# Two-layer fp32 decoder trunk on one core: five FFN groups instead of three, the second product threaded one matmul at a time through the next group's half-width matmuls

## The chip, the core and the metric

The kernel runs on one core of a Trainium2 chip, in one launch. The metric is device time in microseconds (us), the median of the runs. The engines that matter here are TensorE (PE, matrix products), VectorE (DVE, sums and subtractions), ScalarE (ACT, copies, casts and the silu) and SyncE (SP, which issues the loads of the weights). Each engine works through its own queue in order; an instruction that waits for a semaphore holds up all that stands behind it on its engine.

## The reference

Two identical layers work on x, 512 tokens by 1024 channels, in float32. A layer first mixes tokens (attention, retention and a short convolution, gated and summed); this half is untouched by the change. Then comes the feed-forward part (FFN), which is where everything here happens:

```
h  = rmsnorm(x, norm_ffn_g[l])
gu = einsum('bsd,df->bsf', h, w_ffn_in[l])        # 1024 -> 2 * 2816
g, u = gu[..., :2816], gu[..., 2816:]
g  = causal_dwconv(g, ffn_conv_w[l], ffn_conv_b[l])   # 3 taps along the tokens
x  = x + einsum('bsf,fd->bsd', silu(g) * u, w_ffn_out[l])   # 2816 -> 1024
```

The first product (with w_ffn_in) makes g and u; silu(g) times u is called the activation here; the second product (with w_ffn_out) takes it back to 1024 channels and is added to x.

## The kernel before

**Tiling.** x is kept transposed: eight tiles x[0] to x[7] of 128 channels by 512 tokens. The 2816 inner channels are 22 steps of 128. One step f makes one activation tile, act0 to act21, 128 by 512.

**Precision.** Every float32 operand is kept as two parts, hi (rounded) and lo (the rest). A product is three matmuls (function mm3): hi by hi, hi weights by lo data, lo weights by hi data. So each weight tile that is loaded (raw_...) is cast on ACT to hi_... and subtracted on DVE to lo_... (split_w), and the same is done to each activation tile (split2: ACT makes its hi, DVE its lo). A weight pair of more than 512 columns has three buffers (HL), and those of 512 columns two of their own; raw tiles have four.

**First product.** Steps 0 to 4 are `plain`: two products of eight channel tiles each, 48 matmuls of 512 columns. Meanwhile `halves` makes from the normalised x seven half-width combinations X[k][..., b] (256 columns). Steps 5 to 21 are `seven`: a Strassen scheme with seven products instead of eight, each over four channel tiles, thus 7 x 4 x 3 = 84 matmuls of 256 columns per step. Its weights are sums of quarters of the loaded weight (s31 and s24, on DVE, each split again into h31/l31 and h24/l24), the quarter a11 (fa) and the lower half (fb). It uses two PSUM tiles: in `a` (pa) and `b` (pb) the products are collected one after another, and between them ACT copies partial results to `pad` and `u` and DVE adds to them. Within a step the order is: pa with fa, pb with h31, pa with h24, pb with h24, pa with h31, pb with fb, pa with fb. After the first product into pa, ACT copies it to pad (COPY pad), and the third product, into pa again, waits for that copy. When the step's last product of pb is done, the chain to the activation is: pad plus pb (DVE), the convolution (one ACTIVATE on ACT and two on DVE, into c), silu (ACT, c), u times c (DVE), the cast to act hi (ACT), the subtraction to act lo (DVE). The last product, into pa, is copied to u by ACT in between.

**Second product.** The 22 steps are cut into groups of 5, 9 and 8 (GROUPS). After a group, `rows` goes through the eight tiles d: load and split w_ffn_out for this group and d (w2), width x 3 matmuls of 512 columns over the group's activations into one PSUM tile (p2, group, d), and one DVE operation that adds the tile to x[d] (L888). All PSUM tiles pa, pb, p2 come from one pool of four (`main`); a second pool of four (`aux`) is nearly unused in the FFN. In the last group of the last layer each x[d] is written out.

**Order.** The program's text is not the order on the engines: a scheduler, which plans by its own model of times, moves instructions that do not depend on each other, and loads and splits of weights go first (high priority). So before the change matmuls of `rows` stand between matmuls of `seven` wherever the planner saw a wait coming: p200, p201, p202 (group 0, d = 0, 1, 2) are begun together, and each one's last activation is taken later. Instructions marked keep_in_program_order stay in the order of the text on their engine.

Of the kernel before, what the change touches and what calls it, by code (L numbers as in the profile page):

```python
# [15 lines left out]
ALU = mybir.AluOpType  # L16
# [4 lines left out]
P = 128  # L21
D = 1024
S = 512
DEPTH = 2
KT = D // P
# [2 lines left out]
DFF = 2816  # L28
FT = DFF // P

GROUPS = (5, 9, 8)
HALF = S // 2
BUCKETS = 32
MAX_DIST = 128
# [19 lines left out]
def trunk(ctx, tc, xT, wr, wh, wt, wda, wret, wsc, wo, wf, w2, par, lamp, relb, onehot, mask, rope, gtab, out):  # L54
# [99 lines left out]
    def weights(src, name):  # L154
        return split_w(load_w(src, name), name)

    def mm3(o, a, b, start, stop, more=False):

        T.matmul(o, a[0], b[0], start=start, stop=False, skip_group_check=more)  # L159
        T.matmul(o, a[0], b[1], start=False, stop=False, skip_group_check=more)  # L160
        T.matmul(o, a[1], b[0], start=False, stop=stop, skip_group_check=more)  # L161

    def split(src, hi, lo, g=None):

# [602 lines left out]
    def ffn(l, fp):  # L767
# [59 lines left out]
            V.tensor_tensor(u, u, c, ALU.mult)  # L827
            return split2(u, pairN(f"act{f}{L}"))

        def seven(f):  # L830
            upper, lower = [load_w(wf[l, f, :, b * D : (b + 1) * D], f"f{b}{L}{f}") for b in range(2)]
            a21, a11, a22, a12 = upper[:, :S], upper[:, S:], lower[:, :S], lower[:, S:]
            with tc.high_priority():
                w11 = split_w(a11, f"fa{L}{f}")
                s31 = fp.tile([P, 2, S], F32, tag="sum", name=f"s31{f}{L}", bufs=2)
                V.tensor_tensor(s31[:, 0], a21, a11, ALU.add)
                V.tensor_tensor(s31[:, 1], a21, a22, ALU.add)
                h31, l31 = slotX(f"h31{f}{L}"), slotX(f"l31{f}{L}")
                split(s31, h31, l31)
                s24 = fp.tile([P, 2, S], F32, tag="sum", name=f"s24{f}{L}", bufs=2)  # L840
                V.tensor_tensor(s24[:, 0], s31[:, 1], a11, ALU.add)
                V.tensor_tensor(s24[:, 1], s24[:, 0], a12, ALU.add)
                h24, l24 = slotX(f"h24{f}{L}"), slotX(f"l24{f}{L}")
                split(s24, h24, l24)
                w2212 = split_w(lower, f"fb{L}{f}")
            w22, w12 = [tuple(t[:, b * S : (b + 1) * S] for t in w2212) for b in range(2)]

            def product(o, w, b, start, stop):
                for k in range(KT // 2):
                    sl = slice(k * P, (k + 1) * P)  # L850
                    mm3(o, (w[0][:, sl], w[1][:, sl]), (X[k][:, 0, b], X[k][:, 1, b]), start and k == 0, stop and k == KT // 2 - 1, True)

            a = main(f"pa{f}{L}")[:, :HALF]
            b = main(f"pb{f}{L}")
# [19 lines left out]
            V.tensor_tensor(u, u, c, ALU.mult)  # L874
            return split2(u, pairN(f"act{f}{L}"))

        def rows(grp, f0, act, d):

            ps = main(f"p2{grp}{d}{L}")
            width = len(act)  # L880
            edge = min(width, KT // 2) if width > KT else 0
            for a, b in ((0, edge), (edge, width)):
                if a < b:
                    w = weights(w2[l, d, :, (f0 + a) * P : (f0 + b) * P], f"w2{L}{grp}{d}{a}")
                    for n in range(a, b):
                        sl = slice((n - a) * P, (n - a + 1) * P)
                        mm3(ps, (w[0][:, sl], w[1][:, sl]), act[n], n == 0, n == width - 1)
            V.scalar_tensor_tensor(x[d], ps, -1.0 if grp else 1.0, x[d], ALU.mult, ALU.add)  # L888
            if l == DEPTH - 1 and grp == len(GROUPS) - 1:
                nc.sync.dma_start(out[:, d], x[d])  # L890

        f0 = 0
        todo = list(range(KT // 2))
        for grp, width in enumerate(GROUPS):
            act = []
            for f in range(f0, f0 + width):
                act.append(seven(f) if grp else plain(f))
                if f == 1:
                    late.close()
                if grp == 0 and f and todo:  # L900
                    halves(todo.pop(0))
            for d in range(KT):
                rows(grp, f0, act, d)
            f0 += width

    for l in range(DEPTH):
        layer(l)
# [106 lines left out]
```

## Time and profile before

| | |
|---|---|
| median of 3 runs | 1522.4 us (1522.21 to 1522.44) |
| the profiled execution | 1522.98 us, span on the core 1521.2 us |
| PE busy | 1512.6 us, 8510 matmuls |
| PE weight loads busy | 1338.7 us |
| DVE busy | 1105.0 us |
| ACT busy | 734.0 us |
| FFN of layer 0 on PE | from 413.3 to 766.9 us |
| FFN of layer 1 on PE | from 1167.2 to 1517.3 us |

PE's busy time includes the tail of each pipelined matmul, so consecutive matmuls overlap in it. What a matmul costs is better read from the distance between the starts of two that follow each other. The names in the rows are those of the program without their buffer numbers: p200L<-act4L,hi_w2L is the second product of group 0, tile d = 0, with activation 4. In a row of the time order, a bracket at the end gives the idle time of that engine just before, and what released it.

### The profile page before, as it was taken

How to read it: one execution, taken by the hardware profiler on the slowest of the kernel's cores; microseconds unless marked ns; L12 is line 12 of the kernel's file. 1: busy time of each engine (PE TensorE's matmuls, PEld its weight loads, DVE VectorE, ACT ScalarE, POOL GpSimd, SP SyncE). 2: the span in 40 equal slices, each digit the busy share in tenths (PEclk: the TensorE clock that was granted, in tenths of full speed). 3: DMA queues.
4: the chain of work that ended last, by engine and by line, in shares of the span. 5: the costliest groups of instructions: out<-in, count | busy, mean ns of one | idle time of the engine just before them, and what ended most of it. 6: DMA issues, size and time to landing. Idle time of an engine off the chain costs nothing.

```text
span 1521.2 us, 22083 instructions
## 1 busy us (share of the span) xinstructions
PE 1512.6 (99%) x8510; PEld 1338.7 (88%) x8510; DVE 1105.0 (73%) x2074; ACT 734.0 (48%) x1304; POOL 13.0 (1%) x26
## 2 busy tenths in 40 slices
PE   9999999999999999999999999999999999999998
PEld 7899988888888999899789999888888889988996
DVE  8588787554688995796656887875545889947963
ACT  4555665333454564464425565643333546634641
POOL 1000000000000000000100000000000000000000
PEclk9999999999999999999999999999999999999999
DMA  6322222232323322522322222222322233324322
GB/s 212 115 73 81 86 84 90 76 104 83 106 74 107 118 92 72 169 84 84 131 77 94 74 91 87 83 84 83 106 88 86 79 113 112 97 84 139 111 59 81
DMA packets 51146, 147.24 MB, mean 97 GB/s; under 512 B 5624, under 2 KB 6023, under 8 KB 51041
## 3 DMA queue, kind: packets, MB, share of 16 engines
q1 hardware_dynamic: 50224, 143.38, 28.7%
q0 software_dynamic: 816, 2.46, 0.6%
q8 instruction: 67, 1.10, 0.3%
q14 instruction: 39, 0.31, 0.1%
HBM read 143.70 MB, written 2.11 MB: 96 GB/s over the span
## 4 chain that ended last, share of the span: by engine, by line
PE 97%; DVE 1%; DMA 1%; issue 0%; ACT 0%; SPq 0%; ACTq 0%; DVEq 0%
PE pnrvgL L161 1%; PE pnrvgL L159 1%; PE pnrvgL L160 1%; PE pnrqkL L160 1%; PE pnrqkL L161 1%; PE pnrqkL L159 1%; PE pnh2L L161 1%; PE pnh2L L159 1%; PE pnh3L L160 1%; PE pnh3L L161 1%; PE pnh1L L161 1%; PE pnh2L L160 1%; PE pnh3L L159 1%; PE pnh1L L160 1%; PE pnh1L L159 1%; PE pnh0L L160 1%
## 5 line engine op out<-in xcount | busy, mean ns | idle before, releaser
L150 ACT CAST hi_tL<-raw_tL 128x1024 fp32r<-128x1024 f32 x60 | 62.9, 1049 | 115.3 <-issue 14.7
L150 ACT CAST hi_w2L<-raw_w2L 128x640 fp32r<-128x640 f32 (+2 forms) x64 | 49.1, 782 | 94.0 <-PE p210L L160 11.2
L151 DVE TENSOR_TENSOR lo_tL<-raw_tL,hi_tL 128x1024 fp32r<-128x1024 f32 x60 | 73.4, 1223 | 15.9 <-ACT hi_tL L150 15.5
L151 DVE TENSOR_TENSOR lo_w2L<-raw_w2L,hi_w2L 128x640 fp32r<-128x640 f32 (+2 forms) x64 | 55.8, 888 | 29.5 <-ACT hi_w2L L150 29.5
L150 ACT CAST hi_fbL<-raw_f1L 128x1024 fp32r<-128x1024 f32 x34 | 35.7, 1051 | 32.3 <-PE pa5L L160 5.7
L150 ACT CAST hi_oL<-raw_oL 128x1024 fp32r<-128x1024 f32 x16 | 16.9, 1054 | 58.1 <-issue 18.7
L151 DVE TENSOR_TENSOR lo_fbL<-raw_f1L,hi_fbL 128x1024 fp32r<-128x1024 f32 x34 | 41.6, 1222 | 1.5 <-ACT hi_fbL L150 1.4
L150 ACT CAST hi_faL<-raw_f0L 128x512 fp32r<-128x512 f32 x34 | 21.1, 620 | 30.7 <-DMA raw_f0L<-in_wf 12.8
L151 DVE TENSOR_TENSOR lo_faL<-raw_f0L,hi_faL 128x512 fp32r<-128x512 f32 x34 | 23.4, 689 | 4.0 <-ACT hi_faL L150 3.9
L150 ACT CAST hi_nrvgL<-raw_nrvgL 128x1024 fp32r<-128x1024 f32 x8 | 8.4, 1051 | 29.7 <-PE pnrvgL L161 13.5
L150 ACT CAST hi_fuL<-raw_fuL 128x1024 fp32r<-128x1024 f32 x10 | 10.5, 1054 | 22.9 <-issue 17.1
L151 DVE TENSOR_TENSOR lo_oL<-raw_oL,hi_oL 128x1024 fp32r<-128x1024 f32 x16 | 19.6, 1224 | 2.8 <-ACT hi_oL L150 2.8
L151 DVE TENSOR_TENSOR lo_nrvgL<-raw_nrvgL,hi_nrvgL 128x1024 fp32r<-128x1024 f32 x8 | 9.8, 1226 | 12.4 <-ACT hi_nrvgL L150 12.4
L150 ACT CAST hi_fgL<-raw_fgL 128x1024 fp32r<-128x1024 f32 x10 | 10.5, 1050 | 14.8 <-issue 13.0
L151 DVE TENSOR_TENSOR lo_nh0L<-raw_nh0L,hi_nh0L 128x768 fp32r<-128x768 f32 x8 | 7.7, 958 | 13.1 <-ACT hi_nh0L L150 13.1
L150 ACT CAST hi_bdL<-raw_bdL 128x512 fp32r<-128x512 f32 x16 | 9.9, 618 | 12.6 <-issue 4.2
L150 ACT CAST hi_nrqkL<-raw_nrqkL 128x1024 fp32r<-128x1024 f32 (+1 forms) x9 | 8.4, 948 | 13.9 <-issue 13.9
L151 DVE TENSOR_TENSOR lo_fuL<-raw_fuL,hi_fuL 128x1024 fp32r<-128x1024 f32 x10 | 12.2, 1222 | 2.9 <-ACT hi_fuL L150 2.9
L150 ACT CAST hi_nh0L<-raw_nh0L 128x768 fp32r<-128x768 f32 x8 | 6.7, 838 | 15.2 <-PE pnh0L L161 7.8
L151 DVE TENSOR_TENSOR lo_nrqkL<-raw_nrqkL,hi_nrqkL 128x1024 fp32r<-128x1024 f32 (+1 forms) x9 | 9.9, 1109 | 5.2 <-ACT hi_nrqkL L150 5.2
L151 DVE TENSOR_TENSOR lo_fgL<-raw_fgL,hi_fgL 128x1024 fp32r<-128x1024 f32 x10 | 12.2, 1222 | 0.8 <-ACT hi_fgL L150 0.8
L150 ACT CAST hi_nh3L<-raw_nh3L 128x768 fp32r<-128x768 f32 x8 | 6.7, 838 | 11.5 <-PE ptg16L L160 5.3
(8471 smaller groups left out, 5969.6 us busy)
## 6 DMA issues: line engine op xcount, KB each, us to landing
raw_tL<-in_wt SPq DMA_DIRECT2D x60, 512.0 KB, 3.3
raw_f0L<-in_wf SPq DMA_DIRECT2D x34, 512.0 KB, 3.8
raw_f1L<-in_wf SPq DMA_DIRECT2D x34, 512.0 KB, 3.7
raw_w2L<-in_w SPq DMA_DIRECT2D x32, 320.0 KB, 2.9
raw_oL<-in_wo SPq DMA_DIRECT2D x16, 512.0 KB, 3.4
raw_w2L<-in_w SPq DMA_DIRECT2D x16, 512.0 KB, 3.5
raw_fgL<-in_wf SPq DMA_DIRECT2D x10, 512.0 KB, 4.0
raw_fuL<-in_wf SPq DMA_DIRECT2D x10, 512.0 KB, 4.0
```

Source lines behind the costliest of these rows:

```text
L150: A.copy(h, raw)
L151: V.tensor_tensor(w, raw, h.bitcast(F32), ALU.subtract)
L159: T.matmul(o, a[0], b[0], start=start, stop=False, skip_group_check=more)
L160: T.matmul(o, a[0], b[1], start=False, stop=False, skip_group_check=more)
L161: T.matmul(o, a[1], b[0], start=False, stop=stop, skip_group_check=more)
```

## The change

Groups become 5, 4, 4, 4 and 5 steps. `seven` is cut in two: `sums` (the load and the weight sums with their splits) is made for this step and the next before the step's matmuls, and `seven` proper takes an iterator `other`. `rows` is now such an iterator: it yields after each of its matmuls. After every three half-width matmuls (one `product` step over k) `seven` takes one 512-wide matmul from `other`. All matmuls of both kinds are kept in the order of the text. The p2 tiles come from `aux`, and for groups of four one load of 1024 columns serves two tiles d.

After group 0 the tiles d = 0 to 3 run alone (60 matmuls of 512 columns), with the sums of steps 5 and 6 in between; its tiles 4 to 7 (60 matmuls) go between the matmuls of group 1. The 96 matmuls of groups 1, 2 and 3 each go between those of the following group, which has 28 places per step. The last group's 120 run alone at the layer's end. The matmuls are the same in number and size; the additions to x[d] become 80 instead of 48 in the two layers.

```diff
-GROUPS = (5, 9, 8)
+GROUPS = (5, 4, 4, 4, 5)
+SOLID = 4
...
-    def mm3(o, a, b, start, stop, more=False):
-        T.matmul(o, a[0], b[0], start=start, stop=False, skip_group_check=more)
-        T.matmul(o, a[0], b[1], start=False, stop=False, skip_group_check=more)
-        T.matmul(o, a[1], b[0], start=False, stop=stop, skip_group_check=more)
+    def mm3(o, a, b, start, stop, more=False, queue=False):
+        for i, (p, q) in enumerate(((0, 0), (0, 1), (1, 0))):
+            t = T.matmul(o, a[p], b[q], start=start and i == 0, stop=stop and i == 2, skip_group_check=more)
+            if queue:
+                tc.keep_in_program_order(t)
...
-        def seven(f):
+        def sums(f):
             upper, lower = [load_w(wf[l, f, :, b * D : (b + 1) * D], f"f{b}{L}{f}") for b in range(2)]
...
-                w2212 = split_w(lower, f"fb{L}{f}")
+            return lower, w11, h31, l31, h24, l24
+
+        def seven(f, other, lower, w11, h31, l31, h24, l24):
+            w2212 = split_w(lower, f"fb{L}{f}")
...
-                    mm3(o, (w[0][:, sl], w[1][:, sl]), (X[k][:, 0, b], X[k][:, 1, b]), start and k == 0, stop and k == KT // 2 - 1, True)
+                    mm3(o, (w[0][:, sl], w[1][:, sl]), (X[k][:, 0, b], X[k][:, 1, b]), start and k == 0, stop and k == KT // 2 - 1, True, True)
+                    next(other, None)
...
-        def rows(grp, f0, act, d):
-            ps = main(f"p2{grp}{d}{L}")
...
+        def rows(grp, f0, act, ds):
+            width = len(act)
+            per = KT // width
+            for d0 in range(ds.start, ds.stop, per):
...
+                w = split_w(raw, f"w2{L}{grp}{d0}")
+                for d in range(d0, d0 + per):
+                    ps = aux(f"p2{grp}{d}{L}")
+                    for n in range(width):
+                        sl = slice(((d - d0) * width + n) * P, ((d - d0) * width + n + 1) * P)
+                        for i, (p, q) in enumerate(((0, 0), (0, 1), (1, 0))):
+                            t = T.matmul(ps, w[p][:, sl], act[n][q], start=n == i == 0, stop=n == width - 1 and i == 2)
+                            tc.keep_in_program_order(t)
+                            if n < width - 1 or i < 2:
+                                yield
+                    V.scalar_tensor_tensor(x[d], ps, -1.0 if grp else 1.0, x[d], ALU.mult, ALU.add)
...
+                    yield
...
-                act.append(seven(f) if grp else plain(f))
+                if grp:
+                    for n in (f, f + 1):
+                        if n < FT and n not in made:
+                            made[n] = sums(n)
+                    act.append(seven(f, other, *made[f]))
+                else:
+                    act.append(plain(f))
...
-            for d in range(KT):
-                rows(grp, f0, act, d)
+            run(other)
+            if not grp:
+                for half in (range(SOLID // 2), range(SOLID // 2, SOLID)):
+                    run(rows(grp, f0, act, half))
+                    n = f0 + width + half.start // (SOLID // 2)
+                    made[n] = sums(n)
+            other = rows(grp, f0, act, range(0 if grp else SOLID, KT))
             f0 += width
+        run(other)
```

What this does to the queues is seen at three places. A row gives line, operation, what is written <- what is read, and the size; x2 stands for two that read the same. The lines of the changed kernel are shifted: mm3 is L163, the matmul of `rows` L903.

**1. End of group 0 in layer 0.** On PE, p200 is the first tile of the second product and act4 the group's last activation. Before:

```order
L159 MATMUL p200L_4409<-act3L_4302,hi_w2L_4412 128x512
L160 MATMUL p200L_4409<-act3L_4302,hi_w2L_4412 128x512
L161 MATMUL p200L_4409<-act3L_4302,lo_w2L_4413 128x512
L159 MATMUL p201L_4432<-act0L_4050,hi_w2L_4435 128x512
L160 MATMUL p201L_4432<-act0L_4050,hi_w2L_4435 128x512
L161 MATMUL p201L_4432<-act0L_4050,lo_w2L_4436 128x512
```

and now:

```order
L903 MATMUL p200L_4415<-act3L_4302,hi_w2L_4411 128x512 x2
L903 MATMUL p200L_4415<-act3L_4302,lo_w2L_4412 128x512
L903 MATMUL p200L_4415<-act4L_4391,hi_w2L_4411 128x512 x2
L903 MATMUL p200L_4415<-act4L_4391,lo_w2L_4412 128x512
L903 MATMUL p201L_4438<-act0L_4050,hi_w2L_4434 128x512 x2
```

The matmuls on act4 stood behind all of p201's and p202's on the other activations; now they follow act3 directly. On DVE, between u4 times c4 and the lo part of act4, stood before (xt3 and X3 belong to `halves`):

```order
L827 TENSOR_TENSOR u4L_4388<-u4L_4388,c4L_4359 128x512
L800 TENSOR_TENSOR xt3L_4398<-xn3L_4394 128x256
L167 TENSOR_TENSOR X3L_3928<-xn3L_4394,X3L_3928 128x256
L802 TENSOR_TENSOR xt3L_4398<-xn7L_4396,xn3L_4394 128x256
L167 TENSOR_TENSOR X3L_3928<-xn7L_4396,X3L_3928 128x512
L801 SCALAR_TENSOR_TENSOR xt3L_4398<-xt3L_4398,xn7L_4396 128x256
L167 TENSOR_TENSOR act4L_4391<-u4L_4388,act4L_4391 128x512
```

and now:

```order
L831 TENSOR_TENSOR u4L_4388<-u4L_4388,c4L_4359 128x512
L804 TENSOR_TENSOR xt3L_4398<-xn3L_4394 128x256
L841 TENSOR_TENSOR s315L_4463<-raw_f0L_4455 128x512
L842 TENSOR_TENSOR s315L_4463<-raw_f0L_4455,raw_f1L_4457 128x512
L171 TENSOR_TENSOR X3L_3928<-xn3L_4394,X3L_3928 128x256
L806 TENSOR_TENSOR xt3L_4398<-xn7L_4396,xn3L_4394 128x256
L171 TENSOR_TENSOR X3L_3928<-xn7L_4396,X3L_3928 128x512
L805 SCALAR_TENSOR_TENSOR xt3L_4398<-xt3L_4398,xn7L_4396 128x256
L171 TENSOR_TENSOR act4L_4391<-u4L_4388,act4L_4391 128x512
```

The two weight sums of step 5 (s315) have come in ahead of act4's lo part.

**2. From step 12 to step 13, an end of a new group.** On PE, in the middle of step 13 of layer 0, the second product p220 of the group with act9 to act12 now runs between the half-width matmuls:

```order
L903 MATMUL p220L_5813<-act11L_5630,lo_w2L_5810 128x512
L163 MATMUL pa13L_5801<-X1L_3926,h2413L_5651 128x256 x2
L163 MATMUL pa13L_5801<-X1L_3926,l2413L_5652 128x256
L903 MATMUL p220L_5813<-act12L_5772,hi_w2L_5809 128x512
L163 MATMUL pa13L_5801<-X2L_3927,h2413L_5651 128x256 x2
L163 MATMUL pa13L_5801<-X2L_3927,l2413L_5652 128x256
L903 MATMUL p220L_5813<-act12L_5772,hi_w2L_5809 128x512
```

where, before, step 13's third product ran without any between:

```order
L161 MATMUL pa13L_5643<-X0L_3925,l2413L_5636 128x256
L159 MATMUL pa13L_5643<-X1L_3926,h2413L_5635 128x256
L160 MATMUL pa13L_5643<-X1L_3926,h2413L_5635 128x256
L161 MATMUL pa13L_5643<-X1L_3926,l2413L_5636 128x256
L159 MATMUL pa13L_5643<-X2L_3927,h2413L_5635 128x256
```

So the matmul on act12 stands in the order ten places into step 13, with the rest of pa13 and pb13 behind it. On ACT, the chain of act12 before:

```order
L858 COPY pad_116<-pa13L_5643 128x256
L166 CAST h2413L_5635<-s2413L_5632 128x1024
L309 ACTIVATE c12L_5608<-pad_115,par_110 128x512
L166 CAST act11L_5486<-u11L_5389 128x512
L860 COPY u13L_5645<-pb13L_5644 128x256
L150 CAST hi_w2L_5830<-raw_w2L_5828 128x512
L873 ACTIVATE c12L_5608<-c12L_5608 128x512
L150 CAST hi_w2L_5807<-raw_w2L_5805 128x640
L869 COPY u12L_5517<-pa12L_5515 128x256
L862 COPY pad_116<-pa13L_5643 128x256
L166 CAST act12L_5614<-u12L_5517 128x512
```

and now:

```order
L152 CAST hi_w2L_5920<-raw_w2L_5918 128x1024
L878 COPY u12L_5661<-pa12L_5659 128x256
L313 ACTIVATE c12L_5766<-pad_115,par_110 128x512
L152 CAST hi_faL_5952<-raw_f0L_5948 128x512
L867 COPY pad_116<-pa13L_5801 128x256
L869 COPY u13L_5803<-pb13L_5802 128x256
L882 ACTIVATE c12L_5766<-c12L_5766 128x512
L170 CAST act12L_5772<-u12L_5661 128x512
```

The silu of c12 stands behind the copies of pa13 and pb13, as it did before; the consumer of act12 is what moved.

**3. End of layer 0.** On PE, around act21, the last activation. Before:

```order
L161 MATMUL p222L_7161<-act20L_6966,lo_w2L_7165 128x512
L159 MATMUL p220L_7097<-act21L_7094,hi_w2L_7100 128x512
L159 MATMUL p221L_7129<-act21L_7094,hi_w2L_7132 128x512
L159 MATMUL p222L_7161<-act21L_7094,hi_w2L_7164 128x512
L160 MATMUL p220L_7097<-act21L_7094,hi_w2L_7100 128x512
```

and now:

```order
L163 MATMUL pa21L_7075<-X3L_3928,lo_fbL_7072 128x256
L903 MATMUL p240L_7183<-act17L_6593,hi_w2L_7179 128x512 x2
L903 MATMUL p240L_7183<-act17L_6593,lo_w2L_7180 128x512
L903 MATMUL p240L_7183<-act18L_6759,hi_w2L_7179 128x512 x2
L903 MATMUL p240L_7183<-act18L_6759,lo_w2L_7180 128x512
L903 MATMUL p240L_7183<-act19L_6926,hi_w2L_7179 128x512 x2
L903 MATMUL p240L_7183<-act19L_6926,lo_w2L_7180 128x512
L903 MATMUL p240L_7183<-act20L_7068,hi_w2L_7179 128x512 x2
L903 MATMUL p240L_7183<-act20L_7068,lo_w2L_7180 128x512
L903 MATMUL p240L_7183<-act21L_7174,hi_w2L_7179 128x512 x2
```

Between the last half-width matmul (pa21) and the first on act21 there are now exactly 12 matmuls of 512 columns; before, p220, p221 and p222 on all other activations lay around and behind pa21.

19 lines of the change are left out of this document (9 added, 10 removed).

## The prediction

> **What bounds the kernel now.** I read the shares of busy time first, then the chain that ended last:
>
> ```profile
> PE 1512.6 (99%) x8510; PEld 1338.7 (88%) x8510; DVE 1105.0 (73%) x2074; ACT 734.0 (48%) x1304; POOL 13.0 (1%) x26
> ...
> PE 97%; DVE 1%; DMA 1%; issue 0%; ACT 0%; SPq 0%; ACTq 0%; DVEq 0%
> ```
>
> TensorE is busy for 99% of the span and is 97% of the chain. So the change can win only if matmuls follow each other faster, or if PE's few idle moments in the FFN go away; it can lose wherever PE is made to wait. Busy time by stretch (columns: length, busy time and instructions of each engine, granted clock, DMA share, GB/s):
>
> ```profile
> 612.00:637.00 25.00, 25.00 (x112) 20.71 (x111) 19.97 (x27) 9.97 (x12) 0.00 (x0) 1.00 0.48 164
> 640.00:712.00 72.00, 72.00 (x602) 72.00 (x601) 60.83 (x85) 42.51 (x73) 0.00 (x0) 1.00 0.30 96
> 1516.50:1521.20 4.70, 0.73 (x4) 0.27 (x2) 0.69 (x1) 0.00 (x0) 0.00 (x0) 0.85 0.15 56
> ```
>
> The first is a stretch of the second product (512-wide matmuls), the second one of the half-width product, the last the program's end. Half-width matmuls follow each other at 72.00 / 602 = 0.120 us. Weight loads are busy all the time there (72.00 of 72.00) and 83% in the wide stretch. That looks as if a half-width matmul were held by its weight load and a wide one in between could hide it. Starts on PE where the two kinds alternate once, by chance, and at the start of group 0's second product:
>
> ```profile
> 469.16 0.39 PE L159 MATMUL p200L<-act0L,hi_w2L 128*128 128x512 f32 x1
> ...
> 471.88 0.39 PE L159 MATMUL p201L<-act0L,hi_w2L 128*128 128x512 f32 x1
> ...
> 477.32 0.39 PE L159 MATMUL p200L<-act4L,hi_w2L 128*128 128x512 f32 x1
> ...
> 583.27 0.28 PE L159 MATMUL pa13L<-X0L,h2413L 128*128 128x256 f32 x1
> 583.38 0.28 PE L160 MATMUL pa13L<-X0L,h2413L 128*128 128x256 f32 x1
> 583.50 0.40 PE L160 MATMUL p210L<-act10L,hi_w2L 128*128 128x512 f32 x1
> 583.74 0.40 PE L161 MATMUL p210L<-act10L,lo_w2L 128*128 128x512 f32 x1
> 583.97 0.28 PE L159 MATMUL pa12L<-X0L,hi_fbL 128*128 128x256 f32 x1
> ```
>
> From 469.16 to 471.88 there are 12 wide matmuls on act0 to act3: 0.227 us each. Two narrow, two wide (583.27 to 583.97) take 0.70 us; at 0.120 and 0.227 they would take 0.693. So mixing costs what the parts cost apart.
>
> And 0.227 - 0.120 = 0.107 us more for 256 columns more leaves 0.013 us that does not grow with the columns. This is all that a cover over weight loads could win, and the mixed rows show none of it.
>
> **The idle moments that go.** The waits inside the FFN, first of the third product of step 5 in each layer, then the end of the layer:
>
> ```profile
> 501.76 0.39 PE L159 MATMUL pa5L<-X0L,h245L 128*128 128x256 f32 x1 [0.54 <-ACT pad L858]
> ...
> 1256.05 0.39 PE L159 MATMUL pa5L<-X0L,h245L 128*128 128x256 f32 x1 [1.03 <-ACT pad L858]
> ...
> 734.07 0.39 PE L161 MATMUL p222L<-act21L,lo_w2L 128*128 128x512 f32 x1
> ...
> 736.94 0.40 PE L161 MATMUL p223L<-act14L,lo_w2L 128*128 128x512 f32 x1
> ```
>
> The first two are 0.54 and 1.03. From 734.07 to 736.94 lie seven starts, 2.87 us where 7 x 0.227 = 1.59 would do: 1.28 too many, taken as the same in layer 1, which runs the same program. Together 0.54 + 1.03 + 2 x 1.28 = 4.1 us. All are at places that the change reorders, and I count all as removed.
>
> **What is added: waits in a fixed order.** Matmuls, casts and loads of the FFN stay as many; 32 additions to x[d] more on DVE lie beside PE's work. DVE has room in mixed steps: 84 x 0.120 = 10.1 us of narrow matmuls get 28 x 0.227 = 6.4 us of wide ones between them, while the step's sums stay. What costs is that the planner's free order had let other matmuls pass when an activation was late, and a fixed order does not. Everything behind the waiting matmul on PE waits with it.
>
> *A, end of group 0.* act4's hi and lo parts in the trace, on ACT and DVE:
>
> ```profile
> 472.74 0.62 ACT L166 CAST act4L<-u4L 128x512 fp32r<-128x512 f32 x1 [0.71 <-DVE u4L L827]
> ...
> 472.02 0.68 DVE L827 TENSOR_TENSOR u4L<-u4L,c4L 128x512 f32<-128x512 f32 x1
> ...
> 474.56 0.69 DVE L167 TENSOR_TENSOR act4L<-u4L,act4L 128x512 fp32r<-128x512 f32 x1
> ```
>
> Before, p201 and p202 ran from 471.88 until 477.32, and act4 was ready before its turn. Now it is wanted at 471.88, after act3. Its hi part is ready at 472.74 + 0.62 = 473.36: 1.5 us late. The second matmul wants the lo part, 0.227 later. That ended at 475.25, and two sums of 512 columns now stand ahead of it on DVE, each as long as the 0.69 of act4's own: 475.25 + 1.38 = 476.6, 4.5 us after the 472.1 at which the second matmul would have started (471.88 + 0.227). This covers the first wait too, so A is 476.6 - 472.1 = **4.5 us** (1.5 and then 3.0); were the sums done in DVE's idle moments, 475.25 - 472.1 = 3.1. Late next is all of p201 to p203, and with them step 5.
>
> *B, the first threaded tile* (p204, from step 5's first place): its weights' lo part is made after the sums. Not shown before; between 0 and the 1.03 of the wait that stood in this step. I take 0.5, since the load has the solid tiles' time.
>
> *C, copies behind casts.* The third product waits for the copy of the first one; 12 half-width matmuls, 12 x 0.120 = 1.44 us, cover it. The chain of step 21 gives the prices:
>
> ```profile
> 721.00 0.69 DVE L867 TENSOR_TENSOR pad<-pad,pb21L 128x512 f32<-128x512 f32 x1 [1.02 <-PE pb21L L161]
> 722.63 0.75 DVE L310 SCALAR_TENSOR_TENSOR c21L<-pad,par,c21L 128x512 f32<-128x512 f32 x1 [0.94 <-ACT c21L L309]
> 723.42 0.75 DVE L311 SCALAR_TENSOR_TENSOR c21L<-pad,par,c21L 128x512 f32<-128x512 f32 x1
> ...
> 727.28 0.68 DVE L874 TENSOR_TENSOR u21L<-u21L,c21L 128x512 f32<-128x512 f32 x1
> ...
> 721.78 0.82 ACT L309 ACTIVATE c21L<-pad,par 128x512 f32<-128x512 f32 x1 [7.79 <-DVE pad L867]
> 724.21 0.63 ACT L873 ACTIVATE c21L<-c21L 128x512 f32<-128x512 f32 x1 [1.61 <-DVE c21L L311]
> 725.06 1.05 ACT L150 CAST hi_w2L<-raw_w2L 128x1024 fp32r<-128x1024 f32 x1 [0.22 <-PE pa21L L160]
> 726.01 0.37 ACT L869 COPY u21L<-pa21L 128x256 f32<-128x256 f32 x1
> ```
>
> In steps 7, 12 and 16 ACT's order puts a 1024-wide cast (1.05), which waits for a buffer that the threaded tile holds to its end, and a 512-wide cast (0.62, as act4's) ahead of the next step's COPY pad (0.37): 2.04 + about 0.1 against 1.44, so 0.7 late each time, **2.1 us**; from 0, where the buffer comes free early, to 3 (the 1.03 thrice).
>
> *D, ends of groups 1, 2 and 3.* The tenth threaded matmul of the new step wants the last activation. Ten places hold 30 narrow and nine wide matmuls: 30 x 0.120 + 9 x 0.227 = 5.64 us. The bare chain takes 0.69 + 0.82 + 0.75 + 0.75 + 0.63 + 0.68 + 0.62 + 0.69 = 5.6 us to the lo part, about 6 with some 0.1 at each change of engine (721.00 + 0.69 to 721.78). It starts when pb is done, at least 1.44 before the step's end: lo at 4.6, in time. But the silu stands behind COPY u of the next step, which waits for that step's second product: eight places, 24 x 0.120 + 8 x 0.227 = 4.70 us. From there copy 0.37, silu 0.63, u times c 0.68, hi 0.62, lo 0.69 end at 7.7, about 8.2 with the five changes of engine. The lo part is wanted one place after the hi part, at 5.64 + 0.59 = 6.23: **2.0 us** late (the hi part 1.9). Three times: **6.0 us**. From 0, were the silu ahead of the copy, to 3 each, where DVE's sums of step f+2 (0.69 each) come into the chain too.
>
> *E, end of the layer.* From pb's end to the narrow matmuls' end 1.44 us, then 12 wide ones, 2.72 us. The chain has two more items inside: a 640-wide cast of weights ahead of COPY u, and the subtract that goes with it ahead of the last convolution step on DVE:
>
> ```profile
> 469.18 0.73 ACT L150 CAST hi_w2L<-raw_w2L 128x640 fp32r<-128x640 f32 x1 [2.04 <-PE pu4L L160]
> ```
>
> The bare chain of about 6, with 0.3 from pb's end to its start (my estimate, three engine changes) and the cast's 0.73, is at 7.0 us; wanted at 1.44 + 2.72 + 0.227 = 4.4. **2.6 us** late; 1.4 to 3.0 with the two items beside or wholly in the chain.
>
> **Sum.** Per layer 4.5 + 0.5 + 2.1 + 6.0 + 2.6 = 15.7; two layers 31.4; less 4.1 idle time: +27.3. On the profiled execution's 1522.98 that is 1550.3. The median is 0.6 below the profiled execution: about 1549.7. With all low ends (3.1 + 0 + 0 + 0 + 1.4 per layer) it is +4.9, so 1527.3; with the high ends (4.5 + 1.0 + 3 + 9 + 3.0) +36.9, so 1559.3.
>
> **Rivals.**
>
> *Faster: the mix pays.* If one wide matmul hid the fixed 0.013 us of the next narrow one (a start at 0.107 instead of 0.120), 696 threaded matmuls (60 + 3 x 96 per layer) would bring 9 us, and 4.1 us of idle time go as well: 1509. Its place is the threaded steps, its price 0.013 a matmul, and it decides from where the waits A to E stay under 13 us in all. For it speaks the weight loads' 72.00 of 72.00, against it the 0.70 us of the mixed four. The Trainium skill, Perfetto Trace Analysis, section Optimization Strategy, says that where a kernel has regimes with different most-contended engines, interleaving them may help, and the section before it judges TensorE by the weight loads' busy share; by that rule this rival would be the likeliest. The trace disagrees: at 100% weight-load busy the 256-column matmul has the same 0.013 us above its columns as the 512-column one.
>
> *No change: the waits are hidden.* If ACT and DVE run ahead, the late activations are ready when wanted: B, C, D at 0, and A and E shrink to 1 us each, which the removed 4.1 pays in both layers: 1522. For it: ACT is busy only 48%. Against it: D hangs on an order within ACT, not on its load.
>
> *Slower still: the clock.* PE's last work ends at 1516.50 + 0.73 = 1517.2, and the mean clock of 1516.50 to 1521.20 is 0.85; if it halves at one moment, that is 30% of 4.70, so 1.4 us, before the end: at 1519.8, 2.6 us after PE stopped. A's second wait (3.0) reaches this, E just, D at its high end. If the clock then stayed at half for as long (an estimate from that 2.6), each costs 1.3 us: with 4 to 10 such waits +5 to +13, and in the middle 1559. The Trainium skill, TensorE: Matmul & The Clock Gate, section What's actually happening, gives about 3.4 us for the idle window; by it none of these waits would reach the drop, and the sum stays.
>
> *Slower still: another engine's queue.* If loads or DVE get late by the 1.03 us seen before in each of the 17 half-width steps of both layers: 34 x 1.03 = 35 more, 1584. Against it: DVE was at 60.83 of 72.00 in the narrow stretch, and DMA at 0.30.
>
> **Chances.** The forecast 0.69, the clock 0.11, the queue 0.07, no change 0.07, faster 0.06. The forecast, the clock and the queue are slower; of the "no change" case 0.01 falls above. About 0.2% (3 us) is what a measurement here can tell from no change. So faster 0.06, same 0.06, slower 0.88. The forecast's own range is 1530 to 1560. The range 1528 to 1576 takes in the low end of the sum, the clock and a part of the queue case, and leaves out the faster and the unchanged.
>
> **What would show it.** In the new profile: p200 on act4 waiting 1.5 us for ACT and then about 3.0 for DVE, in both layers (A); p210, p220 and p230 on act8, act12 and act16 waiting about 2 us each (D); the pa of the third product waiting for pad after steps 7, 12 and 16 (C); p240 on act21 waiting 2 to 3 us (E); no wait at step 5's pa; PE's busy share below 99%; narrow matmuls after a wide one at 0.12 us, wide ones at 0.23. I am wrong if the pattern of three narrow and one wide takes clearly less or more than 0.587 us, or if the activations stand ready at their tenth place. A clock below 1.00 in any stretch of the FFN would show the third rival.

## The result and the profile after

The changed kernel takes 1560.0 us in the median of five runs (1559.49 to 1560.93) against 1522.4 before (1522.08 to 1523.13): 1.0245 times as long, 95% interval 1.0234 to 1.0257. The forecast was 1549.7, within 1528 to 1576. Direction and range held; the size was 10 us short. The profiled execution took 1559.9 us, span 1558.1.

The shares of busy time and the head of the chain that ended last:

```profile
PE 1528.0 (98%) x8510; PEld 1346.4 (86%) x8510; DVE 1127.8 (72%) x2098; ACT 742.3 (48%) x1296; POOL 13.0 (1%) x26
...
PE 94%; DVE 3%; ACT 1%; issue 1%; DMA 0%; SPq 0%; DVEq 0%; ACTq 0%
```

The number of matmuls is the same, and the chain has 4% of DVE and ACT in it where there was 1%. PE's own busy time grew by 15 us although it does the same work: the matmuls themselves got longer somewhere. First the waits of PE (total, times, the longest of one):

```profile
PE p200L L903 <- DVE act4L L171: 5.2, 2, 2.6
PE p210L L903 <- ACT act8L L170: 3.7, 2, 1.9
PE p230L L903 <- ACT act16L L170: 3.5, 2, 1.8
PE p220L L903 <- ACT act12L L170: 3.5, 2, 1.8
PE p240L L903 <- ACT act21L L170: 3.5, 2, 1.7
PE p200L L903 <- ACT act4L L170: 2.7, 2, 1.4
PE p210L L903 <- DVE act7L L171: 1.9, 2, 0.9
```

Every one is a matmul of the second product that waits for an activation, in both layers, and the waits for pa and p224/p225 of the kernel before are gone. PE's rows in order of time in layer 0 show each place:

```profile
473.16 0.50 PE L903 MATMUL p200L<-act4L,hi_w2L 128*128 128x512 f32 x1 [1.37 <-ACT act4L L170]
476.26 0.75 PE L903 MATMUL p200L<-act4L,hi_w2L 128*128 128x512 f32 x1 [2.60 <-DVE act4L L171]
...
548.68 0.51 PE L903 MATMUL p210L<-act7L,hi_w2L 128*128 128x512 f32 x1 [0.94 <-DVE act7L L171]
...
551.98 0.80 PE L903 MATMUL p210L<-act8L,hi_w2L 128*128 128x512 f32 x1 [1.85 <-ACT act8L L170]
...
618.13 0.50 PE L903 MATMUL p220L<-act12L,hi_w2L 128*128 128x512 f32 x1 [1.75 <-ACT act12L L170]
...
756.92 0.50 PE L903 MATMUL p240L<-act21L,hi_w2L 128*128 128x512 f32 x1 [1.73 <-ACT act21L L170]
757.65 0.50 PE L903 MATMUL p240L<-act21L,hi_w2L 128*128 128x512 f32 x1 [0.23 <-DVE act21L L171]
```

The second thing is the clock. The stretches after the wait at 618.13, and after the same wait in layer 1 at 1391.9:

```profile
618.20:619.70 1.50, 1.50 (x9) 1.33 (x10) 0.60 (x1) 0.00 (x0) 0.00 (x0) 1.00 0.07 27
619.70:623.10 3.40, 3.40 (x15) 3.01 (x14) 0.69 (x1) 0.37 (x1) 0.00 (x0) 0.50 0.02 5
623.10:626.00 2.90, 2.90 (x21) 2.69 (x20) 1.25 (x2) 1.19 (x2) 0.00 (x0) 1.00 0.00 0
1392.00:1395.40 3.40, 3.40 (x22) 3.05 (x23) 1.26 (x2) 0.37 (x1) 0.00 (x0) 1.00 0.03 12
```

For 3.4 us the granted clock is 0.50, and PE does 15 matmuls where it does 22 at full clock. It happens after some waits and not after others of the same length; the last section shows what decides.

**The account.** I added up, over the FFNs of both layers, the distance from each matmul's start to the next, less what its size takes undisturbed (0.227, 0.120). Before it is 6.4 us, after 43.5: 37.1 more, where the profiled executions differ by 1559.9 - 1522.98 = 36.9. Of the 43.5, 27.5 are the waits above (per layer 1.5 + 2.9 for act4, 1.1 for act7, 2.0, 1.9 and 1.9 for act8, act12 and act16, 2.4 for act21). The clock is at half for 24 us in six stretches; outside the waits themselves this costs 10.8 us. About 5 remain, against 6.4 before.

### The profile page after: what moved, and what is told of

Read it like the earlier page. It is cut to its first block, busy times and chain, and to the rows that moved or that the text cites. A ratio compares the mean times of both kernels' runs of the same rounds, so it can differ in the third digit from the quotient of the medians.

```text
span 1558.1 us, 22048 instructions
## 1 busy us (share of the span) xinstructions
PE 1528.0 (98%) x8510; PEld 1346.4 (86%) x8510; DVE 1127.8 (72%) x2098; ACT 742.3 (48%) x1296; POOL 13.0 (1%) x26
## 4 chain that ended last, share of the span: by engine, by line
PE 94%; DVE 3%; ACT 1%; issue 1%; DMA 0%; SPq 0%; DVEq 0%; ACTq 0%
PE pnrvgL L163 3%; PE pnrqkL L163 2%; PE pnh2L L163 2%; PE pnh3L L163 2%; PE pnh1L L163 2%; PE pnh0L L163 2%; PE pb20L L163 1%; PE pb10L L163 1%; PE pa12L L163 1%; PE pa7L L163 1%; PE pa16L L163 1%; PE pa8L L163 1%; PE pa20L L163 1%; PE pa5L L163 1%; PE pa6L L163 1%; PE pb21L L163 1%
## 5 line engine op out<-in xcount | busy, mean ns | idle before, releaser
L152 ACT CAST hi_w2L<-raw_w2L 128x640 fp32r<-128x640 f32 (+1 forms) x56 | 48.5, 866 | 72.6 <-PE pa10L L163 5.9
L153 DVE TENSOR_TENSOR lo_w2L<-raw_w2L,hi_w2L 128x640 fp32r<-128x640 f32 (+1 forms) x56 | 55.4, 990 | 7.2 <-ACT hi_w2L L152 7.2
```

The costliest lines, as they stand in the source:

```text
L152: A.copy(h, raw)
L153: V.tensor_tensor(w, raw, h.bitcast(F32), ALU.subtract)
```

## The experiments

Times are medians; "before" was timed beside each of them at 1522.4 to 1523.0. Ratios carry their 95% interval.

### e1: the solid second products free

```diff
-        def rows(grp, f0, act, ds):
+        def rows(grp, f0, act, ds, fixed=True):
...
-                            tc.keep_in_program_order(t)
+                            if fixed:
+                                tc.keep_in_program_order(t)
...
-                    run(rows(grp, f0, act, half))
+                    run(rows(grp, f0, act, half, False))
...
-            other = rows(grp, f0, act, range(0 if grp else SOLID, KT))
+            other = rows(grp, f0, act, range(0 if grp else SOLID, KT), grp < len(GROUPS) - 1)
```

> One part of the change undone: the second products that run alone (d = 0 to 3 of the first group, and all of the last group) are no longer kept in the order of the text; the threaded ones are. Theory W (waits for late activations, and the halved clock that follows some of them, make the whole loss): p200 no longer waits for act4 (4.4 us per layer in the changed kernel) nor p240 for act21 (2.4), and the halved clock after act4's waits goes (3.3 us at half in layer 0, 6.9 in layer 1, some 4 us lost): 13.6 + 4 = 17.6 less, so 1542. Rival M (the mix of the two kinds of matmul, the groups of four and the extra additions cost by themselves): the waits only hide other delays and at most half comes back, 1550 or more.

Measured: 1561.6 us, 1.0255 (1.0240 to 1.0271). Nothing came back. The waits of PE in this kernel:

```profile
PE p204L L903 <- ACT hi_w2L L152: 7.7, 2, 4.1
...
PE p203L L903 <- DVE lo_w2L L153: 1.5, 2, 0.8
```

The waits for act4 are gone, and p204, the first threaded tile, waits 4.1 us for its weights instead. So the wait for act4 had only stood in front of another. The cast of these weights on ACT, and the wait in the queue of the loads (SPq) ahead of their load:

```profile
487.89 0.72 ACT L152 CAST hi_w2L<-raw_w2L 128x640 fp32r<-128x640 f32 x1 [6.52 <-DMA raw_w2L<-in_w]
```

```profile
SPq L139 <- DVE s245L L846: 3.2, 1, 3.2
```

ACT was not busy here: it stood idle for 6.52 us until the load had landed. The load was issued only at 484.57, when VectorE was done with the first half of s245 (483.85 + 0.69), a weight sum of step 5 that reads a raw tile. VectorE was behind at this place, and the load and the cast were late through it.

### e2 and e3: the threaded matmuls begin 14 places, or 2 places, later

```diff
             act = []
+            if grp:
+                other = chain(repeat(None, 14), other)
             for f in range(f0, f0 + width):
```

(e3 has 2 in place of 14.)

> The threaded matmuls of each group begin 14 places later in the next group (112 or 140 places for 96, so they still fit); all else as changed. Theory W: the waits on act7, act8, act12 and act16 (1.1 + 2.0 + 1.9 + 1.9 per layer, 13.9 in both) vanish, and with them the halved clock after four of them (about 1.65 each, 6.6): 1560 - 20.5 = 1539.5; the waits on act4 and act21 stay. Rival M: the place of the threaded matmuls does not matter, 1555 to 1560. A third way: loads of w2 or the PSUM buffers now collide at the end of the group, a new wait there, and less than half is won.

> The threaded matmuls begin only two places (about 1.2 us) later, which tells how long a wait must be for the clock to halve. Theory W: the waits on act8, act12 and act16 shrink from 1.9 to 2.0 us to about 0.8, the one on act7 goes. If the clock only falls after waits as long as those of the changed kernel (1.9), it stays at 1.00 there and the time is 1560 - 9.2 - 6.6 = 1544; if any wait brings it down, 1551.

Measured: e2 1550.4 us, 1.0178 (1.0161 to 1.0195); e3 1557.6 in one run. In e2 the waits for act7, act12 and act16 are gone, and act8's is down to 0.8. Its waits of PE, apart from those for act4 and act21 that stay:

```profile
PE p210L L904 <- DVE act8L L172: 1.6, 2, 0.8
PE pa7L L164 <- DVE u7L L875: 1.5, 2, 0.8
...
PE p226L L904 <- DVE lo_w2L L154: 0.8, 2, 0.4
PE p216L L904 <- DVE lo_w2L L154: 0.7, 2, 0.4
```

So 9.6 of the 20.5 expected came back. These smaller waits for DVE are 6 of the rest (by the distances of the starts 0.9 + 1.0 + 0.5 + 0.5 per layer). The clock gave some 5 less than expected: it no longer fell in the threaded steps, but it did after act21 in both layers, which it had not done in the changed kernel, and it stayed at half for 6.8 us after act4 in both layers instead of one.

In e3 the waits for act12 and act16 are 1.3 to 1.5 us, and none of the four halved the clock; act8's is 2.5 us and it halved both times. That one grew, though its place moved back: the wait for act7 ahead of it, which had held PE up, was gone, and PE came to act8's place sooner: counted from the start of step 8's last matmul into pb, after 8.1 us instead of 8.6, while act8's hi part was ready after 10.4 us in both.

### e4: both

> Both: solid second products free, threaded ones 14 places later. No matmul should wait for an activation, and the granted clock should be 1.00 through the FFN. Theory W: 1560 - 17.6 - 20.5 = 1522, the time of the kernel before, give or take 2. If removing the idle moments of the kernel before (4.1 us) pays and the mix costs nothing, as low as 1519. Rival M: what the mix, the groups and the additions cost by themselves is left, 1530 or more.

Measured: 1549.0 us, 1.0175 (1.0160 to 1.0190): 11 us of the 38 expected. PE's waits for act4, act12, act16 are gone, and at the start of step 5 there is a new one. PE's rows, and ACT's just before:

```profile
490.54 0.80 PE L164 MATMUL pa5L<-X0L,h245L 128*128 128x256 f32 x2 [3.62 <-ACT h245L L171]
491.80 0.58 PE L164 MATMUL pa5L<-X0L,l245L 128*128 128x256 f32 x1 [0.46 <-DVE l245L L172]
```

```profile
487.61 0.72 ACT L153 CAST hi_w2L<-raw_w2L 128x640 fp32r<-128x640 f32 x1 [1.71 <-DMA raw_w2L<-in_w]
488.24 1.04 ACT L153 CAST hi_fbL<-raw_f1L 128x1024 fp32r<-128x1024 f32 x1
489.18 0.36 ACT L870 COPY u5L<-pb5L 128x256 f32<-128x256 f32 x1
489.45 1.04 ACT L171 CAST h245L<-s245L 128x1024 fp32r<-128x1024 f32 x1
```

The cast of step 5's own sums (h245) stands on ACT behind a cast of w2 that waits for its load. That load was issued at 484.38, again when VectorE was done with the first half of s245. The second half was done at 486.75, and PE stood still from 486.92. Had ACT taken h245 ahead of w2, its 1.04 us would have ended at about 487.8: by this estimate 0.9 of the 3.62 us are VectorE's alone, and the other 2.7 come from the order on ACT behind the late load. In e7 below ACT does take h245 first, and pa5 waits 0.9. VectorE has no time left before it. The stretches 455 to 470 and 470 to 485, before the change and in e4:

```profile
455.00:470.00 15.00, 15.00 (x68) 12.43 (x67) 14.20 (x24) 7.81 (x12) 0.00 (x0) 1.00 0.23 66
470.00:485.00 15.00, 15.00 (x67) 11.87 (x66) 11.67 (x21) 5.85 (x9) 0.00 (x0) 1.00 0.24 67
```

```profile
455.00:470.00 15.00, 15.00 (x68) 12.43 (x67) 14.79 (x24) 8.46 (x13) 0.00 (x0) 1.00 0.28 79
470.00:485.00 15.00, 14.24 (x68) 11.57 (x67) 14.85 (x25) 6.47 (x9) 0.00 (x0) 1.00 0.22 71
```

Before, DVE had caught up after 470 (11.67 of 15), while PE still had 120 wide matmuls of the first group to do. Now the sums of two steps are due within the first 60 of them, and DVE is busy 14.85 of 15.

### e5: the groups alone, in the kernel before

```diff
-GROUPS = (5, 9, 8)
+GROUPS = (5, 4, 4, 4, 5)
```

> The kernel before with one edit: groups of 5, 4, 4, 4, 5 steps, rows and scheduling as before (nothing threaded, nothing fixed, each second product after its group). Theory W2 (what is lost comes from the fixed order and from moving 60 wide matmuls away from the place where VectorE catches up): the groups themselves cost little; more ends of groups of about 1 us each (pa waiting for pad, 0.5 to 1.2 us in the kernel before), two more per layer: 1522 + 4 = 1526, within 1522 to 1530. Rival G (the short groups, with 32 more additions to x and more loads, are what VectorE cannot follow): 1535 or more.

Measured: 1557.2 us, 1.0227 (1.0212 to 1.0242). My expectation failed by 31 us: nothing threaded, nothing fixed, and nearly the whole loss is there. The waits of PE:

```profile
PE p220L L159 <- ACT act12L L166: 3.7, 2, 1.8
PE p230L L159 <- ACT act16L L166: 3.7, 2, 1.8
PE p210L L159 <- ACT act8L L166: 3.7, 2, 1.8
PE pb17L L161 <- DVE l3117L L167: 2.2, 2, 1.1
PE pb13L L161 <- DVE l3113L L167: 2.1, 2, 1.1
PE pb9L L161 <- DVE l319L L167: 2.1, 2, 1.1
```

Each new end of a group costs a wait of 2.0 us for the last activation, and one of 1.1 to 1.3 for the next step's sums; after five of the six waits of 2.0 the clock halved for 3.4 us. So the same places wait as in the changed kernel although the planner was free. In its order between step 8's last matmuls into pb and the one on act8, PE had only p210's and p211's matmuls and the rest of pa8, and then nothing that could pass.

### e6: e4 with the whole first group solid

```diff
-SOLID = 4
+SOLID = 8
```

> As e4, but all eight tiles of the first group's second product run alone before step 5 (120 wide matmuls, 27 us, instead of 60), and none of them is threaded into the second group. Theory W2 (VectorE is behind at this place, busy 14.85 of 15 us until 485, and the 13.6 us of wide matmuls that the change took away were what it caught up in): the wait of pa5 for h245 and l245 (5 us in layer 0, 4.6 in layer 1 with what follows), p203's (0.9) and the half clock after it go: 1549 - 11 - 3 = 1535. If ACT, waiting for a load of w2 ahead of the cast of h245, is the cause and not VectorE, the wait stays near 3 us per layer: 1543 to 1549.

Measured: 1536.2 us, 1.0088 (1.0073 to 1.0103), 12.9 less than e4 and one from the 1535 expected. The wait for h245 is gone (pa5 waits for pad, 2.4 and 1.1 us), the clock is at 1.00 through both FFNs. But the edit does two things at once: it gives back 13.6 us of PE work, and it takes away the load of w2 that stood ahead of h245's cast. Which of the two counts is not separated by it; the rows of e4 above put most of the wait on the cast behind the load, and the load's lateness on VectorE.

### e7 and e8: nothing kept in program order

```diff
             t = T.matmul(o, a[p], b[q], start=start and i == 0, stop=stop and i == 2, skip_group_check=more)
-            if queue:
-                tc.keep_in_program_order(t)
...
                             t = T.matmul(ps, w[p][:, sl], act[n][q], start=n == i == 0, stop=n == width - 1 and i == 2)
-                            tc.keep_in_program_order(t)
```

(e8 has SOLID = 8 as well.)

> The changed kernel with the same text, but no matmul kept in program order: the planner may again move them. Theory W2: the waits for act4, act8, act12, act16 and act21 are passed by other matmuls, but the work that VectorE lacks time for at the end of the first group is the same, as in e4: 1535 to 1550. If the fixed order is all of the loss: 1522 to 1526.

> e7 (nothing kept in program order) with all eight tiles of the first group's second product alone before step 5. Theory W3 (two needs: other matmuls must be free to run while an activation is late, and 27 us of wide matmuls must stand where VectorE catches up after the first group): the waits of p204 (1.8 us with what follows) and pa5 (1.1) per layer and p203's (0.2) go: 1530.4 - 6.2 = 1524, the kernel before within 0.2%. If these waits come from the order of ACT and not from the cover, they stay: 1529 to 1531.

Measured: e7 1530.4 us, 1.0053 (1.0036 to 1.0070); e8 1525.4, 1.0015 (1.0005 to 1.0024). With the same text, the fixed order costs 29.6 us (1560.0 - 1530.4). All waits for activations are gone in e7; what is left is at step 5, and e8 takes that away. The waits of e8 in the FFN:

```profile
PE p203L L901 <- DVE lo_w2L L153: 1.6, 2, 0.8
PE p242L L901 <- ACT hi_w2L L152: 1.4, 2, 0.7
```

That is about as little as before the change. e8 is the fastest of the threaded kernels, and still 0.15% slower than the kernel before.

### e9 and e11: e7's parts without threading

e9 runs each group's second product in the text right after its group; e11 does that with one load per tile d. Against e7:

```diff
-            other = rows(grp, f0, act, range(0 if grp else SOLID, KT))
+            run(rows(grp, f0, act, range(0 if grp else SOLID, KT)))
...
-            per = KT // width
+            per = 1
```

(the second edit in e11 alone)

> e7's kernel (groups of 5, 4, 4, 4, 5, one 1024-column load for two tiles d, p2 in the second PSUM pool, sums two steps ahead, nothing fixed), but each group's second product stands in the text right after the group, as in e5, and nothing is threaded. Theory W3 says that e5 lost because at the end of a group of four only two tiles of the second product had their weights in place: 2 x 9 wide matmuls (4.1 us) against a chain of some 6 us to the last activation. Here four tiles can run, 36 wide matmuls, 8.2 us: the waits for act8, act12 and act16 vanish and the time is near e7's, 1528 to 1534. If threading is what saved e7, it is near e5's 1557, at least 1545.

> e9 with one edit: every load of w2 serves one tile d (512 columns, two buffers for its pair) instead of two tiles (1024 columns, three buffers). If e5 lost because only two tiles' weights were in place at the end of a group (18 wide matmuls, 4.1 us, against the chain to the last activation), the waits for act8, act12 and act16 come back with about 2.0 us each and the clock halves after most of them: 1534 + 12 + 8 = 1554. If the pool for p2 or the earlier sums made e9 fast, nothing changes: 1534.

Measured: e9 1534.0 us, 1.0072 (1.0058 to 1.0086), at the upper end of what was expected; e11 1541.5, 1.0124 (1.0106 to 1.0142), between the two expectations. The waits for act8, act12 and act16 do not come back in e11, though again only p210 and p211 can run. So my account of e5, that the weights of only two tiles were in place, falls. What fills the time in e11 are the first products of step 9, which the planner put ahead of the matmuls on act8: its PE rows show pa9<-h249 between p211 and p210<-act8L, at 549.87. Against e5, e11 has the p2 tiles in the second PSUM pool, the sums made two steps ahead, and those of steps 5 and 6 between the tiles of the first group's second product. e10 speaks only of the pool in the old groups; which of these lets step 9 begin in time stays open. Their longest waits stand at steps 6 and 7: pb6 waits 2.1 to 2.4 us for the cast of step 6's sums, in both layers.

### e10: the p2 tiles in the second PSUM pool, old groups

```diff
-            ps = main(f"p2{grp}{d}{L}")
+            ps = aux(f"p2{grp}{d}{L}")
```

> The kernel before with one edit: the p2 tiles come from the second PSUM pool. If PSUM tiles are what limits the matmuls that may run while an activation is late, the 4.1 us of idle time in its FFN shrink: 1519 to 1521. If it is the weights' buffers, nothing moves: 1522 to 1523.

Measured: 1522.7 us, 0.9996 (0.9987 to 1.0005): no change. PSUM tiles are not what the kernel before lacks.

### e12: SOLID = 8 alone in the changed kernel

> The changed kernel with SOLID = 8 alone (all of the first group's second product ahead of step 5, everything fixed as in the change). If cover and freedom are both needed, cover alone gives little: act4 is wanted at the same place and waits 4.4 us per layer, the waits for act8, act12, act16 and act21 stay: 1553 to 1560. If the cover alone is what counts: 1549 or less.

Measured: 1559.5 us, 1.0245 (1.0227 to 1.0264), as expected. With the fixed order the 13.6 us of cover bring next to nothing: act4 is waited for at the same place (2.87 us for its lo part), and so are the others. In e7, with the order free, the same edit brings 5 us; in e4, where the solid part is free and the threaded part late, 13.

## Why the prediction was right, and where not

**The bound and the mix: right.** PE was full, and mixing matmuls of two sizes won nothing. Undisturbed, a narrow matmul after a narrow one takes 0.119 to 0.120 us in the changed kernel, a narrow one 0.118 before a wide one, and a wide one before a narrow one 0.234 instead of 0.227 (medians of 2158, 690 and 691). A place of three narrow and one wide is thus 0.590 us against the 0.587 of its parts, about 2 us over 696 places: the rival by which the mix pays is out, on the wrong side. One argument against it was empty, though. The 0.013 us was worked out from the difference of the two sizes, so it comes out the same for both whatever holds them. What speaks is the mixed rows.

**A, 4.5 us per layer: right in size and in both parts.** Measured 1.53 + 2.87 = 4.4. The two sums did come between, and act4's lo part ended at 476.20. VectorE's rows:

```profile
472.71 0.68 DVE L841 TENSOR_TENSOR s315L<-raw_f0L 128x512 f32<-128x512 f32 x1
473.31 0.68 DVE L842 TENSOR_TENSOR s315L<-raw_f0L,raw_f1L 128x512 f32<-128x512 f32 x1
...
475.52 0.68 DVE L171 TENSOR_TENSOR act4L<-u4L,act4L 128x512 fp32r<-128x512 f32 x1
```

But its reading was too narrow. e1 shows that the wait stood in front of another of the same size: take it away, and p204 waits. The step that failed there is "DVE has room in mixed steps", with all of the cost put on the fixed order: at the end of the first group VectorE has no room.

**B (0.5) and C (2.1 per layer): did not come.** Neither wait is in the changed kernel. B is missing only because A stands in front of it: once A is gone, in e1, p204 waits 4.1 us (3.7 in layer 1) for its weights, some eight times what I took. The two were added although one hides the other.

C had its cover too small. In steps 13 and 17 four wide matmuls stand between those of the second product, which D counts and C left out: four places are 4 x 0.587 = 2.35 us, not 1.44. Step 13's second product starts at 612.90 and its third at 615.27, and COPY pad was done at 613.63. Against 2.35 the price of 2.14 gives no wait at all. Step 8 has no wide matmuls between; there the cast of w2 began at 533.08, before the first product ended, and COPY pad was done at 535.41, ahead of the third product at 535.88.

**D, 6.0 us per layer: right in size, by a different last link.** Measured 2.0 + 1.9 + 1.9 = 5.8, and 1.1 for act7 that I had not seen. The rows of ACT, then DVE, before the wait at 618.13:

```profile
615.23 0.37 ACT L869 COPY u13L<-pb13L 128x256 f32<-128x256 f32 x1 [1.60 <-PE pb13L L163]
616.07 0.63 ACT L882 ACTIVATE c12L<-c12L 128x512 f32<-128x512 f32 x1 [0.47 <-DVE c12L L315]
617.46 0.62 ACT L170 CAST act12L<-u12L 128x512 fp32r<-128x512 f32 x1 [0.76 <-DVE u12L L883]
```

```profile
614.09 0.68 DVE L153 TENSOR_TENSOR lo_faL<-raw_f0L,hi_faL 128x512 fp32r<-128x512 f32 x1
614.69 0.68 DVE L847 TENSOR_TENSOR s2415L<-s2415L,raw_f1L 128x512 f32<-128x512 f32 x1
615.29 0.74 DVE L315 SCALAR_TENSOR_TENSOR c12L<-pad,par,c12L 128x512 f32<-128x512 f32 x1
```

The silu stands behind COPY u13, as predicted. The copy was done at 615.60, and the silu then waited 0.47 longer for the convolution on DVE, which stood behind a lo part and a sum of step 15. For act16 it was 0.47 too, for act8 1.77. With the copy as the last link, as predicted, the wait for act12 would have been 1.45 (1.92 - 0.47): that the size came out as it did is in part luck. The prediction had DVE's sums only as its high end.

**E, 2.6 us per layer: right.** Measured 1.89 + 0.50 = 2.4.

**The clock: the term that was missing.** The sum had 31.4 us of waits for the two layers; 27.5 came. What it lacked is 10.8 us of matmuls at half clock, which the third rival named at +5 to +13 with a chance of 0.11. Its condition was set too high: I took 2.6 us of standing still, from the end of the program, as what is needed. Waits of 1.9 us were enough in two of the six places for act12, act16 and act21. The 2.6 us is only how far PE's end lay from the end of a window of 3.413 us (last section). With 27.5 + 10.8 + 2 for the mix, less the 4.1 that did go, the sum is 36.2; measured 36.9.

**What the trace of before did not tell.** That the forecast came within 10 us is in part luck, since errors of both signs met: B and C, 5.2 us over the two layers, stood in the sum and did not come; act7 (2.2) and the clock (10.8) came and were not in it. And the sum treated the three parts of the change (groups, threads, fixed order) as one thing, and put the price on the fixed order. e7 says that this is right for the changed text: 29.6 of 37.6 us go with the fixed order alone. e5 says that the groups alone, in the old text, cost 34. These do not add up to the whole because the waits for act8, act12 and act16 are in both, reached in two ways: at the end of a short group PE must have something ready to do while the chain to the last activation runs. The fixed order forbids it, and the old text did not offer it. Early sums, tiles d in the other pool and pairs of loads together offer it when the order is free (e9: 1534.0), and threading in the text then brings another 3.6 (e7: 1530.4). Which of the three is needed, no run shows; e11 does without the pairs of loads at 1541.5.

## What to carry to other kernels

Where PE is 99% busy, an order that mixes two kinds of matmul has almost nothing to win, and each operand that it wants at a fixed place is a wait that nothing can pass: work out for each such place when the operand is ready, by the queues that its chain stands in, and start the threads later than that. Before moving PE work away from a place, look at whether another engine is catching up there: undoing one wait moved it to the next late operand until both the free order and the 120 wide matmuls were back. And a wait of 2 us can cost 1.7 us more, since the clock may halve behind it for 3.4 us.

## What the runs showed of the hardware

I had expected the clock to fall only after some 2.6 us of standing still. Over the FFNs of all profiled executions, a lone wait (nothing else over 0.5 us near it) of up to 1.5 us was never followed by a lower clock, in over fifty cases; of 20 waits of 1.86 to 1.92 us, 7 were; of 16 waits of 1.98 to 2.56 us, 12; of four waits of 3.4 to 4.2 us, all. Every such stretch lasted 3.4 us or twice that (6.8), at a clock of 0.50, and then the clock was at 1.00 at once.

What decides is how the wait falls on a fixed grid. In the ten profiled executions in which the granted clock changes more than once, all 79 changes lie whole multiples of 3.413 us apart within their execution, to within 3 ns. I cut all 14 profiled executions from 50 us on into windows of this grid and added up in each the time in which PE's rows show no matmul. Of the windows at full clock, 6007 had at most 1.57 us of it, and none was followed by a half clock. All 41 with 1.77 us or more were. Of the nine between, at 1.62 to 1.76, five were. So the line lies at about half a window, and the idle time is that of the whole window, not of one wait. After a window at half clock less was enough to stay there: all nine with 0.71 us or more within the programs were followed by another, and none of those with up to 0.55 was.

This settles the wait at 618.13 and the same one at 1391.90. The window that holds the first, and the two that share the second:

```profile
616.28:619.69 3.41, 1.66 (x10) 1.39 (x10) 1.39 (x2) 1.04 (x2) 0.00 (x0) 1.00 0.42 147
1387.69:1391.11 3.42, 2.46 (x17) 2.06 (x15) 2.73 (x5) 1.00 (x2) 0.00 (x0) 1.00 0.80 243
1391.11:1394.52 3.41, 2.62 (x17) 2.37 (x18) 1.47 (x3) 0.99 (x2) 0.00 (x0) 1.00 0.17 66
```

PE is busy for 1.66 of 3.41 us in the first and stands still for 1.75: the clock halves at 619.69. The second wait of 1.75 us is cut in two by the window's edge at 1391.11, into 0.96 and 0.79, and nothing happens. Where the grid lies differs between executions, so which waits are hit is chance; a wait of 1.5 us alone stays under the line wherever it falls. No run moved a wait on the grid on purpose, and the ends of matmuls are modelled in the profile, so the line is no sharper than this.

The Trainium skill, TensorE: Matmul & The Clock Gate, section What's actually happening, has the half clock set in after at least one idle window of about 3.4 us. The length of the stretches agrees with that window; that a whole window must be idle does not agree with the windows that were idle for 1.75 us.
